# A streaming group softmax on one core: one store gives four of its groups to five small DMAs over unequal partition ranges, and the last three tiles change from 20, 16, 4 to 20, 12, 8 groups

## The chip, the cores and the metric

One core of a Trainium2 chip runs the kernel. The metric is the device time of one execution in microseconds (us); less is better. The kernel before took 1333.27 us, the median of three runs (1332.07 to 1334.61). A further execution was taken by the hardware profiler; all rows shown here come from it.

## The reference

The input is float32 of shape (4, 4096, 4352). Each row of 4352 elements is cut into 8 groups of 544, and a softmax is taken in each group:

```
x_g = x.reshape(B, N, 8, 544)
exp = np.exp(x_g - x_g.max(axis=-1, keepdims=True))
out = exp / exp.sum(axis=-1, keepdims=True)
```

So 285.21 MB are read and as many are written, with little arithmetic on each element.

## The kernel before

The tensor is seen as 131,072 groups of 544 floats (2176 bytes). The 128 partitions hold 1024 groups each, and the work is cut into 44 tiles, numbered 0 to 43. Tiles 0 to 40 give 24 groups to each partition (6528 KB a tile), tile 41 gives 20, tile 42 gives 16 and tile 43 gives 4 (line 35). The groups of one partition are contiguous in DRAM, so a tile's transfer is one run of bytes per partition: 52,224 bytes in a full tile. Four SBUF buffers of 24 groups are used in turn (tile t uses buffer t mod 4), and the results overwrite the input in place.

The stages of a tile:

- **Load** (lines 110 to 117). SyncE issues all loads in the order of the tiles. Tile 0 comes in three loads of 8 groups. From tile 4 on, the load of tile t waits until the store of tile t-4 has fully landed (line 116), since both use the same buffer. Loads go through the queue that the profile calls q1.
- **Compute**. VectorE takes the negated maximum of 8 groups at a time (line 77; 4 at a time in the last three tiles, where `ENDING` and `FINE` apply), for all pieces of a tile. ScalarE then does the exponential of each group with its sum (line 100). VectorE takes the reciprocals of the sums (line 85) and multiplies (line 88), piece by piece. VectorE's order is fixed: all maxima of a tile, then all its products, then the next tile. After a tile's last product it raises the semaphore `scaled`.
- **Store**. GpSimd waits for `scaled` and issues the stores of tiles 0 to 41 (line 124), through the queue that the profile calls q0. SyncE issues the stores of the last two tiles, 42 and 43 (line 120), so these go through q1, behind all loads.

A DMA over 128 partitions is carried by the core's 16 DMA engines. Each engine has its own packets, and sends a 4-byte packet of its own to the completion semaphore when its part is done; the semaphore counts 16 of them for each DMA. A load that waits for a store therefore waits for the slowest of the 16 engines.

Of the kernel before, what the change touches and what calls it, by code (L numbers as in the profile page):

```python
# [1 line left out]

# [4 lines left out]


@with_exitstack
def kernel(  # L10
    ctx: ExitStack,
    tc: tile.TileContext,
    x: bass.AP,
    out: bass.AP,
):
    nc = tc.nc
    G = 8
    P = 128
    C = 8
    NT = 4  # L20
    LAST = 2
    FIRST = (8, 8, 8)
    FINE = 4
    ENDING = 3
    f32 = mybir.dt.float32
    X = mybir.AxisListType.X
    Exp = mybir.ActivationFunctionType.Exp
    xf = x.flatten_outer_dims()
    of = out.flatten_outer_dims()
    N, D = xf.shape  # L30
    Dg = D // G
    per = N * G // P
    T = 3 * G
    sizes = [T] * (per // T - 1)
    sizes += [20, 16, per - sum(sizes) - 36]
    nt = len(sizes)
    turns = (nt - 1) // NT
    start = [sum(sizes[:t]) for t in range(nt + 1)]
    assert start[nt] == per and min(sizes) > 0
    xg_all = xf.rearrange("n (g d) -> (n g) d", d=Dg)  # L40
    og_all = of.rearrange("n (g d) -> (n g) d", d=Dg)

    def dram(a, t):
        lo, hi = start[t] * P, start[t + 1] * P
        return a[lo:hi, :].rearrange("(p g) d -> p (g d)", p=P)

    def parts(t):
        size = C if t < nt - ENDING else FINE
        return [(c, min(c + size, sizes[t])) for c in range(0, sizes[t], size)]

    before = [0]
    for t in range(nt):
        before.append(before[-1] + len(parts(t)))

    landed = [tc.alloc_semaphore(f"landed{b}") for b in range(NT)]
    stored = [tc.alloc_semaphore(f"stored{b}") for b in range(NT)]
    first_landed = [tc.alloc_semaphore(f"first_landed{k}") for k in range(len(FIRST) - 1)]
    last_stored = tc.alloc_semaphore("last_stored")
    max_done = tc.alloc_semaphore("max_done")
    exp_done = tc.alloc_semaphore("exp_done")  # L60
    rec_done = tc.alloc_semaphore("rec_done")
    scaled = tc.alloc_semaphore("scaled")

    ctx.enter_context(tc.tile_critical(  # L64
        sync_engine=mybir.EngineType.Pool, no_gpsimd_drain=True))
    bufs = [ctx.enter_context(nc.sbuf_tensor(f"xt{b}", [P, T * Dg], f32)) for b in range(NT)]
    mx = ctx.enter_context(nc.sbuf_tensor("mx", [P, NT, T], f32))
    sm = ctx.enter_context(nc.sbuf_tensor("sm", [P, NT, T], f32))
    rs = ctx.enter_context(nc.sbuf_tensor("rs", [P, NT, T], f32))

    def groups(b, lo, hi):
        return bufs[b][:, lo * Dg:hi * Dg].rearrange("p (g d) -> p g d", d=Dg)

    def vector_tile(t, landed_at, done):
        b = t % NT
        for k, (lo, hi) in enumerate(parts(t)):
            i = nc.vector.reduce_max(  # L77
                out=mx[:, b, lo:hi], in_=groups(b, lo, hi), axis=X, negate=True)
            if t == 0 and k < len(FIRST) - 1:
                i.wait_op(first_landed[k], 16, "sem-ge")  # L80
            elif t == 0 or k == 0:
                i.wait_op(landed[b], landed_at, "sem-ge")
            i.then_inc(max_done, 1)
        for k, (lo, hi) in enumerate(parts(t)):
            nc.vector.reciprocal(out=rs[:, b, lo:hi], in_=sm[:, b, lo:hi]).wait_op(  # L85
                exp_done, done + k + 1, "sem-ge").then_inc(rec_done, 1)
            xg = groups(b, lo, hi)
            i = nc.vector.tensor_tensor(  # L88
                out=xg, in0=xg,
                in1=rs[:, b, lo:hi].unsqueeze(2).to_broadcast([P, hi - lo, Dg]),  # L90
                op=mybir.AluOpType.mult,
            ).wait_op(rec_done, done + k + 1, "sem-ge")
        i.then_inc(scaled, 1)

    def scalar_tile(t, done):
        b = t % NT
        for k, (lo, hi) in enumerate(parts(t)):
            xg = groups(b, lo, hi)
            for g in range(lo, hi):
                i = nc.scalar.activation(  # L100
                    out=xg[:, g - lo, :], in_=xg[:, g - lo, :], func=Exp,
                    bias=mx[:, b, g:g + 1], scale=1.0, accum_out=sm[:, b, g:g + 1])
                if g == lo:
                    i.wait_op(max_done, done + k + 1, "sem-ge")
            i.then_inc(exp_done, 1)

    def buf(t):
        return bufs[t % NT][:, :sizes[t] * Dg]

    for k, size in enumerate(FIRST):  # L110
        cols = slice(sum(FIRST[:k]) * Dg, sum(FIRST[:k + 1]) * Dg)
        nc.sync.dma_start(out=buf(0)[:, cols], in_=dram(xg_all, 0)[:, cols]).then_inc(  # L112
            first_landed[k] if k < len(FIRST) - 1 else landed[0], 16)
    for t in range(1, nt):
        if t >= NT:
            nc.sync.wait_ge(stored[t % NT], 16 * (t // NT))
        nc.sync.dma_start(out=buf(t), in_=dram(xg_all, t)).then_inc(landed[t % NT], 16)
    for t in range(nt - LAST, nt):
        nc.sync.wait_ge(scaled, t + 1)
        nc.sync.dma_start(out=dram(og_all, t), in_=buf(t)).then_inc(last_stored, 16)  # L120

    for t in range(nt - LAST):
        nc.gpsimd.wait_ge(scaled, t + 1)
        nc.gpsimd.dma_start(out=dram(og_all, t), in_=buf(t)).then_inc(stored[t % NT], 16)  # L124
    for t in range(nt - NT, nt - LAST):
        nc.gpsimd.wait_ge(stored[t % NT], 16 * (t // NT + 1))
    nc.gpsimd.drain()
    nc.gpsimd.wait_ge(last_stored, 16 * LAST)

    nc.scalar.preload_act_table(Exp)  # L130
    turn = before[NT]
    with nc.scalar.Fori(0, turns):
        for t in range(NT):
            scalar_tile(t, before[t])
        nc.scalar.sem_inc(max_done, -turn)
    for t in range(turns * NT, nt):
        scalar_tile(t, before[t] - before[turns * NT])

    for t in range(NT):
        vector_tile(t, 16, before[t])  # L140
    for b in range(NT):
        nc.vector.sem_inc(landed[b], -16)
    nc.vector.sem_inc(exp_done, -turn)
    nc.vector.sem_inc(rec_done, -turn)
    with nc.vector.Fori(1, turns):
        for t in range(NT, 2 * NT):
            vector_tile(t, 16, before[t] - turn)
            nc.vector.sem_inc(landed[t % NT], -16)
        nc.vector.sem_inc(exp_done, -turn)
        nc.vector.sem_inc(rec_done, -turn)  # L150
    for t in range(turns * NT, nt):
        vector_tile(t, 16, before[t] - before[turns * NT])


# [1 line left out]
_INS = ['x']  # L156
_OUTS = [((4, 4096, 4352), 'float32')]


# [23 lines left out]
```

## Time and profile before

| what | value |
|---|---|
| median of three runs | 1333.27 us |
| profiled execution, its own time | 1325.78 us |
| its span, first to last instruction | 1323.5 us |
| bytes read, bytes written | 285.21 MB, 285.21 MB |
| DMA rate over the span | 431 GB/s |
| VectorE busy | 1208.0 us (91%) |
| ScalarE busy | 755.2 us (57%) |
| GpSimd busy | 22.6 us (2%) |

The views used below are these. The page's DMA rows give, in 40 equal slices, the mean busy share of the 16 DMA engines in tenths (9 is 90% or more) and the rate. The chain of waits follows the work that ended last back to the start. The DMA view of a window counts the packets that start in that window; "under 512 B" counts the small ones, which here are the 4-byte completion packets, one per engine and DMA. In a window that is short against a packet, shares and rates can exceed what is possible, because a packet is counted whole where it starts; the counts are what such a window is read for. The timeline lists instructions in order of time: start, duration, engine, line, operation, and in brackets the idle time before it with what ended it. "SPq" is SyncE's queue of DMA issues.

### The profile page before, as it was taken

How to read it: one execution, taken by the hardware profiler on the slowest of the kernel's cores; microseconds unless marked ns; L12 is line 12 of the kernel's file. 1: busy time of each engine (PE TensorE's matmuls, PEld its weight loads, DVE VectorE, ACT ScalarE, POOL GpSimd, SP SyncE). 2: the span in 40 equal slices, each digit the busy share in tenths (PEclk: the TensorE clock that was granted, in tenths of full speed). 3: DMA queues.
4: the chain of work that ended last, by engine and by line, in shares of the span. 5: the costliest groups of instructions: out<-in, count | busy, mean ns of one | idle time of the engine just before them, and what ended most of it. 6: DMA issues, size and time to landing. Idle time of an engine off the chain costs nothing.

```text
span 1323.5 us, 2707 instructions
## 1 busy us (share of the span) xinstructions
DVE 1208.0 (91%) x399; ACT 755.2 (57%) x2049; POOL 22.6 (2%) x46
## 2 busy tenths in 40 slices
DVE  7999999999998999999999999889999999999996
ACT  5556666555555556666665555555566566665553
POOL 0000000000000000000000000000000000000000
DMA  9999999999999999999999999999999999999998
GB/s 404 429 429 430 431 437 436 437 429 431 437 432 439 432 429 432 439 432 436 431 431 440 431 439 429 431 436 437 437 431 431 431 437 434 439 431 429 440 431 362
DMA packets 12964, 570.46 MB, mean 431 GB/s; under 512 B 1440, under 2 KB 1440, under 8 KB 1440
## 3 DMA queue, kind: packets, MB, share of 16 engines
q1 hardware_dynamic: 6912, 290.79, 50.9%
q0 software_dynamic: 6048, 279.64, 48.8%
q14 instruction: 4, 0.03, 0.0%
HBM read 285.21 MB, written 285.21 MB: 431 GB/s over the span
## 4 chain that ended last, share of the span: by engine, by line
DMA 72%; DVE 27%; issue 0%; ACT 0%; SPq 0%; POOLq 0%
DMA out_dram<-xt 36%; DMA xt<-in_x_dram 36%; DVE xt L88 14%; DVE mx L77 13%; DVE rs L85 0%; ACT xt L100 0%; SPq L112 0%; SPq L178 0%; POOLq L64 0%; POOLq L167 0%
## 5 line engine op out<-in xcount | busy, mean ns | idle before, releaser
L100 ACT ACTIVATE xt<-xt,mx 128x544 f32<-128x544 f32 x1024 | 749.8, 733 | 554.8 <-DVE mx L77 554.8
L77 DVE TENSOR_REDUCE mx<-xt 128x8 f32<-128x4352 f32 (+1 forms) x133 | 592.4, 4509 | 98.0 <-DMA xt<-in_x_dram 98.0
L88 DVE TENSOR_TENSOR xt<-xt,rs 128x4352 f32<-128x4352 f32 (+1 forms) x133 | 601.3, 4521 | 4.5
L100 ACT ACTIVATION_READ_ACCUMULATOR xt<-xt,mx 128x1 f32 x1024 | 191.4, 187 | 0.0
L124 POOL DMA_DIRECT2D out_dram<-xt x42 | 22.4, 534 | 1262.6 <-DVE xt L88 1262.6
L85 DVE RECIPROCAL rs<-sm 128x8 f32<-128x8 f32 (+1 forms) x133 | 25.6, 193 | 3.1 <-ACT xt L100 3.1
L130 ACT ACT_TABLE_LOAD x1 | 1.3, 1283 | 0.9 <-PEq L167 0.9
L167 POOL MEMSET const-float32-0.0<- 128x1 f32 x1 | 0.1, 98 | 0.2 <-issue 0.2
L167 POOL MEMSET const-bfloat16-1.0<- 128x1 bf16 x1 | 0.1, 101 | 0.0
L167 POOL MEMSET const-float32-1.0<- 128x1 f32 x1 | 0.1, 98 | 0.0
L167 POOL MEMSET const-uint8-127<- 128x1 uint8 x1 | 0.1, 98 | 0.0
## 6 DMA issues: line engine op xcount, KB each, us to landing
out_dram<-xt POOLq DMA_DIRECT2D x41, 6528.0 KB, 48.4
xt<-in_x_dram SPq DMA_DIRECT2D x40, 6528.0 KB, 46.3
xt<-in_x_dram SPq DMA_DIRECT2D x3, 2176.0 KB, 12.5
xt<-in_x_dram SPq DMA_DIRECT2D x1, 5440.0 KB, 43.8
out_dram<-xt POOLq DMA_DIRECT2D x1, 5440.0 KB, 24.3
xt<-in_x_dram SPq DMA_DIRECT2D x1, 4352.0 KB, 40.0
out_dram<-xt SPq DMA_DIRECT2D x1, 4352.0 KB, 14.0
xt<-in_x_dram SPq DMA_DIRECT2D x1, 1088.0 KB, 29.7
```

The costliest lines, as they stand in the source:

```text
L77: i = nc.vector.reduce_max(out=mx[:, b, lo:hi], in_=groups(b, lo, hi), axis=X, negate=True)
L85: nc.vector.reciprocal(out=rs[:, b, lo:hi], in_=sm[:, b, lo:hi]).wait_op(exp_done, done + k + 1, "sem-ge").then_inc(rec_done, 1)
L88: i = nc.vector.tensor_tensor(out=xg, in0=xg, in1=rs[:, b, lo:hi].unsqueeze(2).to_broadcast([P, hi - lo, Dg]), op=mybir.AluOpType.mult,).w ...
L100: i = nc.scalar.activation(out=xg[:, g - lo, :], in_=xg[:, g - lo, :], func=Exp, bias=mx[:, b, g:g + 1], scale=1.0, accum_out=sm[:, b, g:g ...
L124: nc.gpsimd.dma_start(out=dram(og_all, t), in_=buf(t)).then_inc(stored[t % NT], 16)
L130: nc.scalar.preload_act_table(Exp)
L167: nc = _bacc.Bacc("TRN2", target_bir_lowering=False, num_devices=1)
```

## The change

There are two edits.

The last three tiles hold 20, 12 and 8 groups instead of 20, 16 and 4.

The store of tile 20 is split. The first 20 of its 24 groups go out in one DMA over 128 partitions. The last 4 groups (8704 bytes in each partition) go out in five DMAs over partitions 0 to 1, 2 to 101, 102 to 103, 104 to 105 and 106 to 127. The first four of the five are cut into runs of 2 groups (`max_dma_last_dim`, 4352 bytes); the fifth has runs of 8704 bytes. All six DMAs raise the same semaphore, and the load of tile 24 now waits for all six (`stored_by`).

```diff
+    UNEVEN = (20,)
+    EDGE = 4
+    PIECE = 2
+    SPLITS = ((0, 2), (2, 102), (102, 104), (104, 106))
...
-    sizes += [20, 16, per - sum(sizes) - 36]
+    sizes += [20, 12, per - sum(sizes) - 32]
...
+    def stores_of(t):
+        return 2 + len(SPLITS) if t in UNEVEN else 1
+
+    def stored_by(t):
+        return 16 * sum(stores_of(u) for u in range(t % NT, t + 1, NT))
+
     for t in range(1, nt):
         if t >= NT:
-            nc.sync.wait_ge(stored[t % NT], 16 * (t // NT))
+            nc.sync.wait_ge(stored[t % NT], stored_by(t - NT))
...
     for t in range(nt - LAST):
         nc.gpsimd.wait_ge(scaled, t + 1)
-        nc.gpsimd.dma_start(out=dram(og_all, t), in_=buf(t)).then_inc(stored[t % NT], 16)
+        o, i, done = dram(og_all, t), buf(t), stored[t % NT]
+        if t not in UNEVEN:
+            nc.gpsimd.dma_start(out=o, in_=i).then_inc(done, 16)
+            continue
+        edge = (sizes[t] - EDGE) * Dg
+        nc.gpsimd.dma_start(out=o[:, :edge], in_=i[:, :edge]).then_inc(done, 16)
+        for lo, hi in SPLITS:
+            nc.gpsimd.dma_start(
+                out=o[lo:hi, edge:], in_=i[lo:hi, edge:],
+                max_dma_last_dim=PIECE * Dg * 4).then_inc(done, 16)
+        rest = SPLITS[-1][1]
+        nc.gpsimd.dma_start(out=o[rest:, edge:], in_=i[rest:, edge:]).then_inc(done, 16)
     for t in range(nt - NT, nt - LAST):
-        nc.gpsimd.wait_ge(stored[t % NT], 16 * (t // NT + 1))
+        nc.gpsimd.wait_ge(stored[t % NT], stored_by(t))
```

Where the instructions stand is read in each engine's program. The first place is GpSimd's list of stores (`out_dram<-xt`; the shape is partitions by elements, or partitions by runs by elements). Before, its rows around the stores are:

```order
L178 UNCONDITIONAL_BRANCH
L124 DMA out_dram<-xt 128x13056 x41
L124 DMA out_dram<-xt 128x10880
L112 UNCONDITIONAL_BRANCH
L64 UNCONDITIONAL_BRANCH
```

After the change the same place reads:

```order
L136 DMA out_dram<-xt 128x13056 x20
L139 DMA out_dram<-xt 128x10880
L141 DMA out_dram<-xt 2x2x1088
L141 DMA out_dram<-xt 100x2x1088
L141 DMA out_dram<-xt 2x2x1088 x2
L145 DMA out_dram<-xt 22x2176
L136 DMA out_dram<-xt 128x13056 x20
L136 DMA out_dram<-xt 128x10880
```

One store in the middle of 41 equal ones has become six, and no wait stands between the six.

The second place is the list of SyncE's DMAs, loads (`xt<-in_x_dram`) and the last two stores. Before:

```order
L112 DMA xt<-in_x_dram 128x4352 x3
L117 DMA xt<-in_x_dram 128x13056 x40
L117 DMA xt<-in_x_dram 128x10880
L117 DMA xt<-in_x_dram 128x8704
L117 DMA xt<-in_x_dram 128x2176
L120 DMA out_dram<-xt 128x8704
L120 DMA out_dram<-xt 128x2176
```

After:

```order
L116 DMA xt<-in_x_dram 128x4352 x3
L127 DMA xt<-in_x_dram 128x13056 x40
L127 DMA xt<-in_x_dram 128x10880
L127 DMA xt<-in_x_dram 128x6528
L127 DMA xt<-in_x_dram 128x4352
L130 DMA out_dram<-xt 128x6528
L130 DMA out_dram<-xt 128x4352
```

The order is the same; four groups per partition have moved from tile 42 to tile 43, in the load and in the store. On VectorE tile 42 has three maxima and three products instead of four and four, and tile 43 two and two instead of one and one.

## The prediction

> **What bounds the kernel now.** I read the page's engine rows first, then its DMA rows, then the chain.
>
> ```profile
> DVE 1208.0 (91%) x399; ACT 755.2 (57%) x2049; POOL 22.6 (2%) x46
> DMA  9999999999999999999999999999999999999998
> GB/s 404 429 429 430 431 437 436 437 429 431 437 432 439 432 429 432 439 432 436 431 431 440 431 439 429 431 436 437 437 431 431 431 437 434 439 431 429 440 431 362
> DMA 72%; DVE 27%; issue 0%; ACT 0%; SPq 0%; POOLq 0%
> ```
>
> The 16 DMA engines are busy in every slice; VectorE, the next busiest, is idle for 9% of the span. The DMA view of the stretch from 400 to 1200 us says how busy, and what a packet costs:
>
> ```profile
> DMA packets 7478, 347.14 MB, mean 434 GB/s; under 512 B 831, under 2 KB 831, under 8 KB 831
> q0 software_dynamic: 3743, 173.75, 50.2%
> q1 hardware_dynamic: 3735, 173.39, 50.0%
> ```
>
> 50.2% and 50.0% are all of 16 engines times 800 us. So the kernel is bound by bytes through the engines, and its floor is the work of the engine that has most. 100.2% x 16 x 800 us over 7478 - 831 = 6647 packets of 52,224 bytes is 1.930 us a packet. Since no byte is saved, only two things are left to change: how evenly the engines end, and pauses at the end.
>
> How evenly they end is read from the completion packets ("under 512 B"). Four windows: 1305.2 to 1306.29 and 1308.7 to 1308.8 us (store of tile 41, q0), 1319.3 to 1319.62 and 1321.6 to 1321.7 us (store of tile 43, q1):
>
> ```profile
> DMA packets 14, 0.04 MB, mean 40 GB/s; under 512 B 13, under 2 KB 13, under 8 KB 13
> ...
> DMA packets 2, 0.03 MB, mean 348 GB/s; under 512 B 1, under 2 KB 1, under 8 KB 1
> ...
> DMA packets 16, 0.03 MB, mean 82 GB/s; under 512 B 13, under 2 KB 13, under 8 KB 13
> ...
> DMA packets 1, 0.00 MB, mean 0 GB/s; under 512 B 1, under 2 KB 1, under 8 KB 1
> ```
>
> Thirteen engines finish tile 41 by 1306.25 us, and the last one at 1308.75; the whole kernel ends with the last one alone at 1321.65, two us after the thirteen. The two others, by the same count (one completion each), finish tile 41 in these windows, 1306.6 to 1306.8 and 1308.0 to 1308.2 us:
>
> ```profile
> DMA packets 2, 0.03 MB, mean 174 GB/s; under 512 B 1, under 2 KB 1, under 8 KB 1
> ```
>
> So there are three **late engines**, at 1306.75, 1308.1 and 1308.75. Before the store of tile 42 the thirteen pause: in 1306.44 to 1306.6 us thirteen first packets of q1 start together.
>
> ```profile
> q1 hardware_dynamic: 13, 0.45, 658.1%
> ```
>
> **The change part by part.** First the five extra DMAs. GpSimd issues them after the store of tile 20, here with the next store; the third row is SyncE's issue of the loads of tiles 23 and 24, the second of which ends at 691.99.
>
> ```profile
> 643.35 0.53 POOL L124 DMA_DIRECT2D out_dram<-xt  x1 [30.29 <-DVE xt L88]
> 674.16 0.53 POOL L124 DMA_DIRECT2D out_dram<-xt  x1 [30.28 <-DVE xt L88]
> 660.86 31.13 SPq L117 DMA_DIRECT2D xt<-in_x_dram  x2
> ```
>
> Five more issues at 0.53 us are 2.7 us on GpSimd, inside 30.28 us in which it only waits: nothing. Without that idle time the store of tile 21 would go out 2.7 us later.
>
> The smaller packets: from 1317.9 to 1319.3 us (store of tile 43, 8704 bytes a packet) the engines gave
>
> ```profile
> q1 hardware_dynamic: 65, 0.55, 93.5%
> ```
>
> which is 93.5% x 16 x 1.4 us over 63 data packets, 0.332 us each. With 1.930 us for 52,224 bytes, a packet costs 0.012 us and 36.7 ns for each 1000 bytes. An unsplit row of the last 4 groups then costs 0.32 us within its long packet, as two runs of 4352 bytes 0.34 us, as one of 8704 bytes 0.33 us. No row shows a 4352-byte packet; 0.17 us is an estimate from those two. Spread evenly, 234 more packets x 0.012 us over 16 engines are 0.18 us.
>
> The main term is **who carries the 128 rows**. Before, each engine carries 8 of them, 2.56 us. No row shows a DMA of 2, 22 or 100 partitions. What binds from below: the latest engine can be spared at most its 8 rows, 2.6 us. From above: all 100 rows on one engine are 92 rows more, 92 x 0.34 = 31 us. The nearest rows are the 128-partition DMAs, where all engines used carry equal parts. I take equal parts here too: 100 rows on ten engines (the largest number up to 16 that divides 100) at 10 rows, 2 rows on two engines, 22 rows on eleven at 2 rows. If the first four DMAs use different engines (2 + 10 + 2 + 2 = 16), about ten engines end with up to 12 rows, 10 x 0.34 + 2 x 0.33 = 4.1 us, or 1.55 us more than before; six engines end with 1 to 3 rows, 0.34 to 1.0 us, or 1.55 to 2.2 us less.
>
> The Trainium skill, "DMA: Bandwidth & Descriptors", section "Why a DMA increments its semaphore by 16 and not by 1", gives the dividing rule for the number of engines, but also an exception that speaks against it: some direct copies from GpSimd run on all 16 with the rows rounded up. By the exception 100 rows are 7 on fourteen engines, 2 on the fifteenth, none on the last, and only the last two are clearly spared; no row of this case shows either form.
>
> Next, the **order of packets**. In the window 1286 to 1296 us loads of 8704-byte packets run beside stores of much larger ones, and both queues start about as many packets (q1's 94 hold 16 completions):
>
> ```profile
> q0 software_dynamic: 87, 3.39, 78.3%
> q1 hardware_dynamic: 94, 0.82, 19.3%
> ```
>
> An engine alternates packet by packet. So a small store packet lets a whole load packet of 1.93 us pass. When the store of tile 20 starts, at about 661 us, some 12 load packets are ahead on each engine (half of tile 22, all of 23). Eight go beside the eight long store packets (8 x (1.61 + 1.93) = 28.3 us), four beside the first four small ones (8.4 us), and the other 18 small ones follow alone (3 us): tile 20 is stored at about 701 us where it was 691.5, while load 23 lands 7 to 9 us earlier. Load 24 is issued later, and the load queue may run dry for 4 us. What covers this is the store of tile 21, issued at 674.16 and waiting in q0; no engine stands still, so it costs nothing. Without that cover it would cost those 4 us.
>
> Last, the **tail**. Load and store bytes are the same, four groups move one tile on. VectorE before:
>
> ```profile
> 1285.99 9.40 DVE L77 TENSOR_REDUCE mx<-xt 128x4 f32<-128x2176 f32 x4 [1.35 <-DMA xt<-in_x_dram]
> 1305.49 2.41 DVE L77 TENSOR_REDUCE mx<-xt 128x4 f32<-128x2176 f32 x1
> 1311.00 0.18 DVE L85 RECIPROCAL rs<-sm 128x4 f32<-128x4 f32 x1 [3.10 <-ACT xt L100]
> 1311.22 2.43 DVE L88 TENSOR_TENSOR xt<-xt,rs 128x2176 f32<-128x2176 f32 x1
> ...
> 1273.09 0.33 SPq L117 DMA_DIRECT2D xt<-in_x_dram  x1
> 1305.60 8.41 SPq L120 DMA_DIRECT2D out_dram<-xt  x2
> ...
> xt<-in_x_dram SPq DMA_DIRECT2D x1, 1088.0 KB, 29.7
> ```
>
> Tile 42 ends one maximum (2.35 us) and one product with its reciprocal (2.55) sooner, and starts 1.35 us sooner, since its smaller load has landed: its store is issued at about 1299.4 instead of 1305.60, and the pause of the thirteen goes. Load 43 lands at 1273.09 + 29.7 = 1302.8 at the latest; the wait for it takes the place of the wait for load 42. From there two maxima, eight exponentials and the last product take 2.45 + 8 x 0.73 + 0.2 + 2.6 = 11.1 us, so store 43 is issued at 1313.9, against 1313.7 before. A store started 0.84 us after its issue above (1305.60 to 1306.44), so it can start at 1314.75. An engine that has finished tile 41 at x ends the store of tile 42 (12 groups, 8 x 0.97 us) at x + 7.7. The latest is busy until 1316.4, so its end does not move: for it, nothing; for the thirteen, a pause of up to 1.5 us. Left alone, the tail is worth 0; if the final chain were later by more than 1.7 us, it would set the end.
>
> **The sum.** If the latest two engines are spared, their ends fall to 1308.75 - 1.55 = 1307.2 or less, and the fullest of the others rises to 1306.25 + 1.55 = 1307.8. The engine that ends last then does so 0.95 us earlier, and 20 groups follow for all as before. 1307.8 + 7.7 = 1315.5 is behind 1314.75, so no new pause opens. Forecast: span 1322.55, own time 1324.8. The runs without the profiler took 1333.27, 7.5 us more than the profiled 1325.78, and no row says where; I take the difference over: 1333.27 - 0.95 = **1332.3 us**.
>
> **The rivals.**
>
> - *The latest engine is among the fuller ones* (the other side). It decides as soon as 4 more rows fall on the engine that ends at 1308.75: 1308.75 + 1.55 = 1310.3, price 1.55 us, 1334.8. For it: nothing names that engine, and ten of sixteen are fuller. Against: it needs only to be one of six.
> - *The latest is spared, the second is not.* 1308.1 + 1.55 = 1309.65, price 0.9 us, 1334.2. It holds if the late engines are not neighbours in the engines' numbering, as the spared ones would be. The Trainium skill, same page, section "Latency and other measured facts", says that engines 7 and 15 are usually slower, half the row apart; the trace agrees that a few are late, but does not name them.
> - *The change does not do what it says*: the pieces are spread over all engines about evenly, or rounded up. Price 0.1 to 0.2 us, 1333.4.
> - *The 100 rows fall on few engines.* On five engines 20 rows each, 12 x 0.34 = 4.1 us more: 1306.25 + 4.1 - 1308.75 = 1.6 us, 1334.9, if on-time ones; on a late one 4.1, 1337.4; on one engine 31 us, 1364. For it: no row excludes it; against: every DMA of the trace gives 16 equal parts.
>
> **How the numbers follow.** Latest two spared 0.36, latest fuller 0.18, second fuller 0.16, about even 0.20, few engines 0.05, something unseen 0.05. That spared beats fuller is my judgement, not a row; the six would hold the latest by chance in 6 cases of 16. The best case, all three late engines brought to the thirteen, cannot give more than 1308.75 - 1306.25 = 2.5 us. The three runs lie 1.3 us to each side of their median, and I add that at both ends: 1332.3 - 2.0 = 1330.3, and 1334.8 + 1.3 = 1336.1. About 0.2% (2.7 us) is what a measurement of this kernel can tell from no change. Nearly every case lies within it: same 0.70. Faster takes a full relief and a favourable median, 0.15; slower takes few engines, or the fuller latest and an unfavourable median, 0.15.
>
> **What the new profile would show.** Store of tile 20: completions spread over several us, its last at about 700, load 24 issued then, load 23 landed near 698. If small packets do not alternate one by one, these two move by less than 3 us, and the sum stays. At the end: if spared, the completions of the last store lie closer than 2.2 us, and most engines end together; if the latest is fuller, one engine alone ends 3 us or more after the pack. SyncE issues store 42 by 1300. I am wrong if the engines stand idle anywhere between 690 and 1300 us, or if one engine takes tens of us more than the others.

## The result and the profile after

The changed kernel took 1330.57 us (median of 6 runs, 1329.63 to 1334.75), the kernel before beside it 1332.66 (6 runs, 1326.1 to 1334.61): ratio 1.0001, 95% interval 0.9975 to 1.0028. That is the "same" that was forecast, 1.7 us below the forecast of 1332.3. But two later comparisons of the same pair, with more runs, tell it apart from no change: ratio 1.0028 [1.0010, 1.0047] and 1.0031 [1.0011, 1.0050], so **some 4 us slower** where the prediction worked out 0.95 us faster. The two profiled runs differ by 4.85 us: 1325.78 us before (span 1323.5), 1330.63 after (span 1328.9).

Single runs of one program lie up to 12 us apart, which hid this at first; the section on the experiments shows for one run what made it long. The lowest runs lie closer: 1325.6 to 1326.5 in six sets of runs of the kernel before, 1328.6, 1329.6 and 1329.6 in three sets of the changed one, whose 25 runs hold none below 1328.6.

Where the time went is read first from the page after: its rate by slices of 33.2 us, its packets and its queues.

```profile
GB/s 403 426 429 434 437 432 432 435 434 435 431 435 434 435 431 437 432 432 432 435 423 406 437 434 431 434 437 434 432 431 439 434 432 431 437 435 434 433 428 337
DMA packets 13493, 570.47 MB, mean 429 GB/s; under 512 B 1734, under 2 KB 1734, under 8 KB 1946
```

Two slices in the middle stand out, 423 and 406 (664 to 731 us), where every slice of before between the second and the last but one has 429 or more. The split store starts there. The same stretch in the view by windows, first before, then after; the last two columns are the share of 16 engines that was busy and GB/s:

```profile
660.00:740.00 80.00, 72.47 (x24) 43.20 (x118) 1.59 (x3) 1.00 1.01 436
740.00:1250.00 510.00, 468.53 (x149) 296.10 (x805) 8.50 (x16) 1.00 1.00 434
```

```profile
660.00:740.00 80.00, 69.98 (x23) 42.91 (x118) 1.65 (x3) 1.00 1.00 417
740.00:1250.00 510.00, 467.72 (x149) 293.18 (x797) 8.50 (x16) 1.00 1.00 434
```

After 740 us the rate is the same. Between 660 and 740 us the engines are as busy (1.00) and move 19 GB/s less: (436 - 417) / 434 x 80 us = 3.5 us of the 4.85 by which the two profiled runs differ. Engines that are busy and move less have slower packets; they don't stand idle. Another 1.05 us are at the end: the windows 1323.1 to 1323.5 and 1326.4 to 1326.6 us of after show

```profile
DMA packets 14, 0.02 MB, mean 44 GB/s; under 512 B 13, under 2 KB 13, under 8 KB 13
...
DMA packets 1, 0.00 MB, mean 0 GB/s; under 512 B 1, under 2 KB 1, under 8 KB 1
```

Thirteen engines have ended by 1323.4, the last ends at 1326.5, 3.1 us behind; before it was 2.05 us. So the engines end less evenly than before, not more.

The order of packets changed the way that was predicted. SyncE's issue of load 24 after, then VectorE's maxima:

```profile
703.45 0.33 SPq L127 DMA_DIRECT2D xt<-in_x_dram  x1
```

```profile
703.25 13.86 DVE L81 TENSOR_REDUCE mx<-xt 128x8 f32<-128x4352 f32 x3
...
741.14 4.68 DVE L81 TENSOR_REDUCE mx<-xt 128x8 f32<-128x4352 f32 x1 [9.51 <-DMA xt<-in_x_dram]
```

Load 24 is issued at 703.45 us, when the last piece of store 20 has landed (forecast about 701). Tile 23 is there early (its maxima at 703.25 wait for nothing), and VectorE waits 9.51 us for tile 24. No packet of a load starts from 694.5 to 708.1 us: the load queue is dry for 13.6 us, where the forecast had 4. The store of tile 21 was to cover that.

### The profile page after: what moved, and what is told of

Read it like the earlier page. It is cut to its first block, busy times and chain, and to the rows that moved or that the text cites. A ratio compares the mean times of both kernels' runs of the same rounds, so it can differ in the third digit from the quotient of the medians.

```text
span 1328.9 us, 2712 instructions
## 1 busy us (share of the span) xinstructions
DVE 1207.9 (91%) x399; ACT 755.2 (57%) x2049; POOL 25.8 (2%) x51
## 2 busy tenths in 40 slices
DMA packets 13493, 570.47 MB, mean 429 GB/s; under 512 B 1734, under 2 KB 1734, under 8 KB 1946
## 4 chain that ended last, share of the span: by engine, by line
another core or an unknown queue 42%; DMA 35%; DVE 20%; issue 1%; SPq 1%; ACT 0%; DVEq 0%; POOLq 0%
DMA out_dram<-xt 18%; DMA xt<-in_x_dram 17%; DVE xt L92 10%; DVE mx L81 10%; ACT xt L104 0%; SPq L127 0%; DVE rs L89 0%; SPq L116 0%; DVEq L163 0%; DVEq L166 0%; SPq L199 0%; POOLq L68 0%; DVEq L165 0%; DVEq L164 0%
## 5 line engine op out<-in xcount | busy, mean ns | idle before, releaser
L136 POOL DMA_DIRECT2D out_dram<-xt x41 | 22.0, 537 | 1232.0 <-DVE xt L92 1232.0
L141 POOL DMA_DIRECT2D out_dram<-xt x4 | 2.5, 631 | 0.1
L139 POOL DMA_DIRECT2D out_dram<-xt x1 | 0.5, 531 | 30.2 <-DVE xt L92 30.2
L145 POOL DMA_DIRECT2D out_dram<-xt x1 | 0.5, 545 | 0.0
```

Of the source, the lines that this page charges most:

```text
L136: nc.gpsimd.dma_start(out=o, in_=i).then_inc(done, 16)
L139: nc.gpsimd.dma_start(out=o[:, :edge], in_=i[:, :edge]).then_inc(done, 16)
L141: nc.gpsimd.dma_start(out=o[lo:hi, edge:], in_=i[lo:hi, edge:], max_dma_last_dim=PIECE * Dg * 4).then_inc(done, 16)
L145: nc.gpsimd.dma_start(out=o[rest:, edge:], in_=i[rest:, edge:]).then_inc(done, 16)
```

## The experiments

Four sets; the kernels of a set ran on one chip beside the same runs of the kernel before. The table gives what was measured; the expectations stand with each kernel below.

| kernel | runs | median, lowest us | ratio to before [95%] | GB/s 660 to 740 us | 740 to 1250 |
|---|---|---|---|---|---|
| c1 before again | 10 | 1330.18, 1326.51 | 0.9996 [0.9972, 1.0020] | 435 | 433 |
| e1 tail sizes alone | 10 | 1328.69, 1325.98 | 0.9998 [0.9976, 1.0020] | 435 | 434 |
| e2 split store alone | 10 | 1330.23, 1329.72 | 1.0009 [0.9988, 1.0030] | 420 | 434 |
| e3 small packets, even | 10 | 1329.79, 1326.98 | 0.9994 [0.9969, 1.0018] | 435 | 434 |
| c2 after again | 10 | 1331.65, 1328.62 | 1.0028 [1.0010, 1.0047] | 422 | 433 |
| e4 split at tile 40 | 10 | 1333.13, 1328.73 | 1.0036 [1.0013, 1.0058] | 435 | 434 |
| e5 rows of 8704 bytes | 10 | 1330.69, 1326.67 | 1.0024 [1.0004, 1.0044] | 426 | 433 |
| e6 others spared, tile 40 | 8 | 1331.12, 1329.10 | 1.0034 [1.0007, 1.0061] | 437 | 434 |
| c3 after a third time | 9 | 1332.29, 1329.55 | 1.0031 [1.0011, 1.0050] | 422 | 434 |
| e7 whole rows, 112+8+8 | 4 | 1401.97, 1344.27 | none (one of 1344, three of 1390 to 1414) | 403 | 411 |
| e8 112 rows, edges cut | 4 | 1338.07, 1336.96 | 1.0081 [1.0064, 1.0097] | 412 | 431 |
| e9 as e3, runs set to 2176 bytes | 10 | 1329.37, 1326.30 | 0.9993 [0.9969, 1.0018] | 435 | 434 |

The kernel before had, in the four sets, 31, 29, 14 and 13 runs with medians 1328.21, 1328.16, 1327.65 and 1329.54 us and lowest 1325.64, 1325.74, 1325.84 and 1325.95.

### First set: which half of the change

**c1**: the kernel before, unedited, for the noise.

> This is the kernel before, unchanged, profiled a second time. Theory 'spread' (most of the 5.4 us between the two profiled spans is run-to-run spread of one program): the span of this profile lies anywhere between 1323 and 1333 us, and the rate in the window 660 to 740 us is again about 434 to 436 GB/s. Theories 'order of packets' and 'placement' (below) say nothing against that, but need the window at 434 to 436 GB/s and a distance of about 2 us between the thirteenth and the last engine at the end here too.

Nothing differs, as it must; but its profiled run took 1335.93 us, 10 more than the fastest of the kernel before. The DMA view of 1312.8 to 1318.9 us and of 1318.9 to 1319.3 us shows why:

```profile
DMA packets 33, 1.18 MB, mean 193 GB/s; under 512 B 0, under 2 KB 0, under 8 KB 0
q0 software_dynamic: 3, 0.13, 4.9%
...
q0 software_dynamic: 1, 0.00, 0.1%
```

By 1312.6 us fifteen engines have ended the store of tile 41 (in q0). Then q0 has three data packets in 6.1 us, one behind the other on one engine, whose completion comes at 1319.1: one engine is 6.5 to 9.7 us late, and the end waits for it. So a run's time can hold the accident of one late engine. It isn't the only one: when the load of tile 21 lands, at about 643 us, ahead of any split store's packets, the last engine is 5.4 to 8.7 us behind the first in the profiled runs of c1, c2, c3 and e5 (by the load's 16 completion packets), and at most 3.3 us behind in the ten others. Those four took 1332.7 to 1335.9 us; of the others only e7 and e8 took more than 1331. The rate in the window 660 to 740 us is free of this (435 in c1), and tells a loss of 2 us better than a median of ten runs.

**e1**: the tail sizes alone, all stores plain.

```diff
-    sizes += [20, 16, per - sum(sizes) - 36]
+    sizes += [20, 12, per - sum(sizes) - 32]
```

> Only the sizes 20, 12, 8; every store is one DMA. All theories: 434 to 436 GB/s from 660 to 740 us. The tail moves the store of tile 42 about 6 us earlier, and should leave the end of the latest engine where it was: time within 0.1% of before. If the tail is what hurts (its last chain from the landing of load 43 sets the end), the thirteen engines pause by more than 1 us before the last store and the time is 1 to 3 us longer.

0.9998, and 435 GB/s in the window: the tail neither costs nor gains. Store 42 is issued at 1299.61 us here, as forecast (1299.4).

**e2**: the split store alone; the diff of e1 undone in the changed kernel.

> Only the split store of tile 20; the tail is 20, 16, 4. 'Order of packets' (small store packets each let a long load packet pass, loads run ahead, the load queue runs dry near 700 us and the engines lose some 3 us): about 417 GB/s from 660 to 740 us, as in the changed kernel. 'Placement' (the three late engines are among those that got 12 rows): at the end the last engine is 3.5 us or more behind the thirteenth, against about 2 us before. 'Spread': 434 GB/s in the window and 2 us at the end.

Its ratio doesn't settle it (1.0009, interval from -0.1 to +0.3%), its window does:

```profile
660.00:740.00 80.00, 70.93 (x25) 43.90 (x120) 1.66 (x3) 1.00 1.00 420
```

(436 - 420) / 434 x 80 us = 2.9 us are lost there, and its lowest run is 1329.72, where 18 of the 31 runs of the kernel before are below that. The split alone brings the loss.

**e3**: the last 4 groups in one DMA over all 128 rows, in the same runs of 4352 bytes. Every engine then has 16 small packets.

```diff
-    SPLITS = ((0, 2), (2, 102), (102, 104), (104, 106))
+    SPLITS = ((0, 128),)
...
-        return 2 + len(SPLITS) if t in UNEVEN else 1
+        return 1 + len(SPLITS) if t in UNEVEN else 1
...
-        rest = SPLITS[-1][1]
-        nc.gpsimd.dma_start(out=o[rest:, edge:], in_=i[rest:, edge:]).then_inc(done, 16)
```

> As the changed kernel, but the last 4 groups of tile 20 go out in one DMA over all 128 partitions with the same runs of 4352 bytes: small packets, even shares. 'Order of packets': 16 small packets per engine instead of up to 22 with their completions; the store of tile 20 still lands several us late, and the window 660 to 740 us still shows less than 430 GB/s. 'Placement': the window may be slow, but the last engine ends about 2 us behind the thirteenth as before. If the unequal shares or the unused engines are what slows the window, it is back at 434 GB/s here.

```profile
660.00:740.00 80.00, 74.55 (x26) 44.44 (x122) 1.63 (x3) 1.00 1.01 435
```

Nothing is lost. It isn't the 4352-byte packets as such, and not that they are many; it is something that comes with the pieces over fewer than 128 partitions.

### Second set: the place, the size of the runs, the engines spared

**c2**: the changed kernel again.

> The changed kernel, unchanged, once more. 'Order of packets' and 'placement': the window 660 to 740 us again shows about 417 to 420 GB/s, the lowest runs lie at 1329.6 us or above, some 4 us over the lowest runs of before (1325.6), and the last engine ends 2.5 us or more behind the thirteenth. 'Spread': its lowest runs come down to 1326 to 1327 us and the window is not low every time.

1.0028 [1.0010, 1.0047], 422 GB/s in the window. The change costs 1 to 6 us.

**e4**: the same split on the store of tile 40, whose buffer no load waits for.

```diff
-    UNEVEN = (20,)
+    UNEVEN = (40,)
```

> The same split on the store of tile 40 instead of tile 20. No load waits for that store. 'Order of packets': the late store holds nothing up, the load queue does not run dry, so the 3 us of the window are gone and the lowest runs are at 1327 to 1328 us (1325.6 plus 1.5 for the larger share on the latest engine). 'Placement' alone, without a cost of the order: 1330 us as with tile 20, and 434 GB/s everywhere. The window 660 to 740 us is at 434 to 436 GB/s by every theory.

1.0036, lowest 1328.73: as slow as with tile 20, but by another road. Its windows, then those of e1, which has the same tail:

```profile
660.00:740.00 80.00, 72.19 (x24) 43.71 (x120) 1.59 (x3) 1.00 1.01 435
1250.00:1310.00 60.00, 58.52 (x35) 35.14 (x96) 4.17 (x7) 1.00 1.00 424
```

```profile
660.00:740.00 80.00, 72.41 (x26) 43.90 (x120) 1.60 (x3) 1.00 1.01 435
1250.00:1310.00 60.00, 54.87 (x33) 32.15 (x89) 1.07 (x2) 1.00 0.99 429
```

The stretch at tile 20 is whole again and the one at tile 40 has the dip. It holds only (429 - 424) / 434 x 60 = 0.7 us of the 2.75 between the lowest runs of e4 and e1. The rest lies in how unevenly the engines end: the 16 completions of the last store come from 1318.0 to 1325.6 us in e4 and from 1320.7 to 1322.4 in e1, on average at 1321.0 and 1321.1. With the split at tile 20 the average itself is later: 1323.8 in the changed kernel against e1's 1321.1, and 1323.8 in e2 against 1319.8 before, each pair with the same tail. So e4 doesn't show that the loss at tile 20 comes without a load that is issued late.

**e5**: the pieces in whole rows of 8704 bytes, half as many packets.

```diff
-    PIECE = 2
+    PIECE = 4
```

> As the changed kernel, tile 20, but the last 4 groups go out in one run of 8704 bytes per row: about 15 small packets per engine instead of 28, if the rows fall on the engines as before. 'Order of packets': like the even small packets, 16 per engine, which kept 435 GB/s, the window 660 to 740 us recovers to 430 GB/s or more. If unequal shares or idle engines make the window slow, it stays at 417 to 422. 'Placement': the last engine still ends 2.5 to 3.5 us behind the thirteenth, lowest runs about 1327 us. If two-dimensional pieces are spread over all 16 engines with the rows rounded up, the number of 4-byte packets falls well below the changed kernel's 1734.

```profile
660.00:740.00 80.00, 76.91 (x26) 49.87 (x136) 1.46 (x3) 1.00 1.01 426
```

426 GB/s is 1.8 us lost, and 1.0024: between the changed kernel and before. This isn't a test of the number of packets alone, since the rows also went to other engines. The page counts the 4-byte packets, of before, of after (above) and of e5:

```profile
DMA packets 12964, 570.46 MB, mean 431 GB/s; under 512 B 1440, under 2 KB 1440, under 8 KB 1440
```

```profile
DMA packets 13237, 570.47 MB, mean 428 GB/s; under 512 B 1584, under 2 KB 1584, under 8 KB 1584
```

Five more DMAs have 80 completions. What goes beyond, 1734 - 1440 - 80 = 214 and 1584 - 1440 - 80 = 64, fits to the packet if an engine without a share gets as many 4-byte packets as the others have data packets: 214 = 14 x 2 + 6 x 20 + 14 x 2 + 14 x 2 + 5 x 2 with the pieces on 2, 10, 2, 2 and 11 engines; 64 = 14 + 14 + 14 + 10 + 12 if the 100 whole rows go 7 each to fourteen engines, 2 to the fifteenth and none to the last. So the prediction's equal parts hold for the change, and rounding up, which it set aside there, holds for e5.

**e6**: e4 with six pieces and a rest of 16 partitions, which by the same rule spare other engines (positions 5 to 10 of the 16).

```diff
-    SPLITS = ((0, 2), (2, 102), (102, 104), (104, 106))
+    SPLITS = ((0, 25), (25, 31), (31, 56), (56, 81), (81, 87), (87, 112))
```

> Tile 40 again, with pieces of 25, 6, 25, 25, 6, 25 and 16 partitions. If 25 rows go on five engines and 6 on six, in turn, the six engines 5 to 10 in that order get 3 rows instead of 8 (-1.6 us) and the other ten 11 rows (+1.0 us); in the changed kernel positions 0, 1 and 12 to 15 were spared, and the latest engine was one of positions 2 to 10. 'Placement': with the latest engine spared more often, the last engine ends nearer to the thirteenth than in the run with the changed kernel's pieces on tile 40, and the lowest runs are 1.5 to 2.5 us below that run's. If placement does not matter, both have the same lowest runs within 0.5 us.

1.0034 beside e4's 1.0036, lowest runs 1329.10 and 1328.73. If the loss came from the fuller engine being the late one, sparing others would have moved it by 1.5 to 2.5 us. The lowest runs differ by 0.4 us, and the last store's completions are as far apart (1318.2 to 1326.1 us). But its window is slower than e4's:

```profile
1250.00:1310.00 60.00, 58.53 (x35) 34.03 (x93) 5.47 (x9) 1.00 1.00 417
```

(424 - 417) / 434 x 60 = 1.0 us could hide a gain of that size. So sparing other engines gains no 1.5 us, and nothing can be said below about 1 us.

### Third set: no small packets

**c3**: the changed kernel a third time.

> The changed kernel, a third time, in five rounds, to say whether it is slower than before or the same. 'Order of packets' with 'placement' expects 1.002 to 1.004 times the time of before, lowest runs at 1328.6 to 1329.6 us. 'Spread' expects a ratio within 0.1% of one.

1.0031 [1.0011, 1.0050], as c2.

**e7**: three DMAs of whole rows (52,224 bytes) over 112, 8 and 8 partitions, no small packet at all.

```diff
-    SPLITS = ((0, 2), (2, 102), (102, 104), (104, 106))
+    SPLITS = ((0, 112), (112, 120), (120, 128))
...
+            nc.gpsimd.dma_start(out=o[lo:hi], in_=i[lo:hi]).then_inc(done, 16)
```

> Tile 20 again, but without small runs: the store goes out in three DMAs of whole rows (52,224 bytes), over 112, 8 and 8 partitions. If 112 rows are 7 on each engine and 8 rows are one on each of the first eight engines, both times, eight engines carry 9 rows (+1.93 us) and eight 7 (-1.93 us). Long packets only, so 'order of packets' expects no loss: 430 GB/s or more from 660 to 740 us. 'Placement': the lowest runs are 1.9 us above those of before (1325.7) if the latest engine is among the first eight, so about 1327.6, with the last engine 4 us behind the thirteenth; if it is among the other eight the lowest runs are within 0.5 us of before. If unequal shares by themselves slow the window, it is at 417 to 425 GB/s here too. If the two 8-row DMAs take different halves, nothing differs from before.

The largest loss of all, 1344 to 1414 us; the profiled run is one of the three long ones, 1390.21. The page's rate by slices, then the windows:

```profile
GB/s 409 421 436 431 434 433 433 433 433 433 433 433 435 433 433 433 433 433 435 400 396 412 429 423 429 426 417 430 430 429 417 390 388 397 375 381 362 314 266 325
```

```profile
660.00:740.00 80.00, 65.86 (x23) 44.09 (x120) 1.12 (x2) 1.00 1.00 403
740.00:900.00 160.00, 144.09 (x48) 88.35 (x240) 2.65 (x5) 1.00 1.00 422
900.00:1100.00 200.00, 158.86 (x51) 98.41 (x267) 3.19 (x6) 1.00 0.99 420
1100.00:1250.00 150.00, 121.45 (x39) 78.26 (x214) 2.12 (x4) 1.00 0.94 388
```

Up to 1100 us the engines are as busy as before and carry less, long after the one split store; later they stand idle too. Nothing recovers, though every later DMA is over 128 partitions. What lasts is one late engine: by its completions the load of tile 39 lands on fourteen engines from 1217.4 to 1218.3 us, on one at 1226.5 and on the last at 1252.8, 35 us late, where the load of tile 21, ahead of the split, had all within 3.0 us. Why that engine fell behind isn't shown, nor whether it did in the run of 1344.27. No small packet is needed for the loss in the first window.

**e8**: 112 whole rows, then twice 8 rows, each cut into one group and 23.

```diff
+        nc.gpsimd.dma_start(out=o[:112], in_=i[:112]).then_inc(done, 16)
...
+            for c0, c1 in ((0, Dg), (Dg, sizes[t] * Dg)):
+                nc.gpsimd.dma_start(
+                    out=o[lo:hi, c0:c1], in_=i[lo:hi, c0:c1],
+                    max_dma_last_dim=(c1 - c0) * 2).then_inc(done, 16)
```

> The mirror: 112 whole rows, then for two times 8 rows one group (two runs of 1088 bytes) and 23 groups (two runs of 25,024 bytes). If three-dimensional pieces of 8 rows take eight engines in turn, the two 23-group pieces both fall on the last eight engines: these carry about 8.9 rows (+1.8 us), the first eight about 7.1 (-1.8 us). 'Placement' expects the opposite of the run with the lower half fuller: one of the two has its lowest runs 1.5 to 2 us above the other's, and the one with the latest engine spared ends with less than 1 us between the thirteenth and the last engine. 'Order of packets': 4 more short or half-long packets per engine and queue, so at most 1 us lost in the window 660 to 740 us.

```profile
660.00:740.00 80.00, 70.40 (x23) 43.32 (x118) 1.67 (x3) 1.00 1.00 412
740.00:1250.00 510.00, 460.22 (x146) 285.65 (x777) 8.50 (x16) 1.00 1.00 431
```

1.0081: 412 GB/s are 5 to 10 below the changed kernel's 417 to 422, and the rest runs at 431 instead of 434. Its 4-byte packets don't tell which half of the engines got the fuller share, so it can't say whether the half matters, as it was meant to.

e7 and e8 say something else. From 664 to 684 us the only store under way is their first piece, 112 whole rows. e7's 4-byte packets (1488 = 1440 + 32 completions of two more DMAs + 16) leave no engine without a share of it: the two pieces of 8 rows take the 16, one for each of the 8 engines without a row. So the 112 rows are 7 on each engine. Before, e7 and e8:

```profile
664.00:684.00 20.00, 17.52 (x7) 6.87 (x21) 0.53 (x1) 1.00 1.01 439
...
664.00:684.00 20.00, 16.38 (x7) 5.74 (x17) 0.58 (x1) 1.00 1.00 402
...
664.00:684.00 20.00, 15.97 (x7) 5.32 (x15) 0.58 (x1) 1.00 1.00 397
```

The twelve other profiled runs have 431 to 452 GB/s there. So a piece over 112 partitions slows the packets with equal shares, long packets only, and before any load is issued late.

### Last: the order by itself

One rival was left: in e3 the load queue's gap (8.1 us, from 696.6 to 704.7) is shorter than in the changed kernel (13.6 us). **e9** was to make it longer without uneven shares: e3 with runs of one group.

```diff
-    PIECE = 2
-    SPLITS = ((0, 2), (2, 102), (102, 104), (104, 106))
+    PIECE = 1
+    SPLITS = ((0, 128),)
```

> Even shares, but twice as many small packets: the last 4 groups of tile 20 in one DMA over 128 partitions with runs of 2176 bytes, 32 small packets per engine, as many turns as the changed kernel's 28 and their completions. 'Order of packets' alone: the store of tile 20 lands as late as in the changed kernel, no load packet starts for 10 us or more near 700 us, and the window 660 to 740 us falls to 417 to 424 GB/s; ratio 1.001 to 1.003. 'Rows carried by other engines' (new: what slows the packets is that the pieces are laid on other engines than those that carry these rows in a 128-partition DMA, and that the engines fall out of step): the load queue may run dry just as long, but the window keeps 430 GB/s or more and the time is that of before within 0.1%.

It didn't. The pages of e3 and of e9 count the same packets:

```profile
DMA packets 13236, 570.46 MB, mean 429 GB/s; under 512 B 1456, under 2 KB 1456, under 8 KB 1712
...
DMA packets 13236, 570.46 MB, mean 430 GB/s; under 512 B 1456, under 2 KB 1456, under 8 KB 1712
```

The last 4 groups of 128 rows are in 1712 - 1456 = 256 packets in both, so they have 4352 bytes, 16 on each engine, though runs of 2176 were set. e9 is e3 once more: load 24 is issued at 700.88 us (e3 701.06), the gap is 8.2 us, and the time is again that of before. The window, then the DMA view of 690 to 720 us of e9 and of after:

```profile
700.88 0.33 SPq L127 DMA_DIRECT2D xt<-in_x_dram  x1
```

```profile
660.00:740.00 80.00, 74.52 (x26) 43.98 (x120) 1.60 (x3) 1.00 1.01 435
```

```profile
DMA packets 503, 12.77 MB, mean 426 GB/s; under 512 B 33, under 2 KB 33, under 8 KB 279
```

```profile
DMA packets 742, 11.87 MB, mean 396 GB/s; under 512 B 303, under 2 KB 303, under 8 KB 514
```

So a load queue that is dry for 8 us costs nothing that shows, while the store of tile 21 is there. For the 13.6 us of the changed kernel that is not shown. There is a sign that the gap has a part. These are the first sixteen load packets behind it, in after (708 to 711.3 us) and in e9 (704.5 to 706.7 us):

```profile
q1 hardware_dynamic: 16, 0.84, 88.5%
...
q1 hardware_dynamic: 16, 0.84, 92.8%
```

Sixteen packets and a share of 16 engines make 88.5% x 3.3 us = 2.92 us a packet in after, and 92.8% x 2.2 us = 2.04 us in e9, where 1.93 is usual: 0.99 us lost on each engine against 0.11.

## Why the prediction was right or wrong

**GpSimd: right.** The five issues lie in its waiting time, which for the store of tile 21 falls from 30.28 to 27.19 us:

```profile
643.01 0.53 POOL L139 DMA_DIRECT2D out_dram<-xt  x1 [30.21 <-DVE xt L92]
643.62 2.52 POOL L141 DMA_DIRECT2D out_dram<-xt  x4
646.13 0.55 POOL L145 DMA_DIRECT2D out_dram<-xt  x1
673.86 0.58 POOL L136 DMA_DIRECT2D out_dram<-xt  x1 [27.19 <-DVE xt L92]
```

**More packets: not contradicted.** 0.18 us would not be seen, and e3 and e9 show no loss; a packet of 4352 bytes usually takes 168 ns there (0.17 us forecast). **Equal parts: right**, by the 214 fill packets. The dividing rule of the Trainium skill, "DMA: Bandwidth & Descriptors", section "Why a DMA increments its semaphore by 16 and not by 1", agrees with this count, and its exception with e5's 64.

**The order of packets: right in direction, too small in size, its price open.** Load 24 is issued at 703.45 us (forecast about 701), but the load queue is dry for 13.6 us, not 4. The step "no engine stands still, so it costs nothing" holds for the gap of 8 us in e3 and e9. In the changed kernel no engine stood still either, but the first packets behind the gap were slow, 0.99 us on each engine, and the step had no term for that.

**The tail: right, worth 0** (e1). In the changed kernel the store of tile 42 is issued at 1302.19 instead of the forecast 1299.4 (e1 1299.61), since everything runs later:

```profile
1302.19 15.31 SPq L130 DMA_DIRECT2D out_dram<-xt  x2
```

**Who carries the rows: here the prediction failed.** The step was "ten engines end with up to 12 rows, 10 x 0.34 + 2 x 0.33 = 4.1 us, or 1.55 us more than before", and behind it "If the latest two engines are spared". It priced a row at 0.34 us whichever engine carries it and whatever the others do. Each engine's packets can be followed through the trace, as each starts where the last one ended. The time of its packets beyond the usual price (the most frequent time of a size, 1.928 us for 52,224 bytes), averaged over the 16 engines, between 660 and 740 us: before 0.01 us, e9 0.26, e3 0.35, e5 1.60, e2 2.48, after 2.42, of which 0.63 lies in the small packets and 1.79 in long ones. Of its 212 packets of 4352 bytes 30 took over 200 ns, sixteen of them 311 to 346 ns, about twice the usual 168. Of the 1.79 us only 0.24 are in packets that start by 703.1 us, when the last piece has ended; 0.42 are in store packets behind that and 1.12 in load packets, most of it in the first sixteen of load 24. The other three traces of this split (e2, c2, c3) have 1.5 us behind the last piece too. So the piece that failed is one that no row of the profile before could show: when a store is cut over fewer than 128 partitions, packets get slower, its own and long ones of both queues, and most of the time lost in long ones is lost when its pieces are done. In place of -0.95 us the runs have some +4 (c2 +3.5 and c3 +4.6 between the medians).

**"Latest two spared": not so.** In the profiles of the changed kernel and of e2, the engine that was latest before the split is, by its count of small packets, one of the fuller, and the end is 3.1 us wide. This was the rival "the latest engine is among the fuller ones", priced at 1.55 us. But the end explains only about 1 us of the profiled 4.85; the other 3.5 are lost around the split. The sum had also left out the third late engine: had only that one been fuller, 1306.75 + 1.55 = 1308.3 us would have left 0.45 of the 0.95 us.

**The range** was to hold 1330.57, and did; the later medians, 1331.65 and 1332.29, lie in it too. What it was put around was wrong: 1333.27, the median of the three runs shown, was high by chance; the later sets of 13 to 31 runs have 1327.65 to 1329.54. The forecast's error in sign and this offset nearly cancelled, so that it came within 1.7 us is luck. The 7.5 us that it carried over between profiled and other runs were spread of single runs: the lowest runs without the profiler are at 1325.6 too.

**What stays open** is why pieces over fewer than 128 partitions slow packets. In a transfer to 128 partitions, says the Trainium skill, same page, section "The descriptor swizzle", each engine writes one SBUF port of its own. If stores read it in the same way, a piece that hands rows to other engines could put two engines at a port. The 112 rows of e7 and e8, slow with equal shares, fit that, but no trace names engines or ports, so it is argued and not shown. It would not explain the packets that are slow behind the last piece. For these the dry load queue is a rival: no run on tile 20 had such pieces without a late load 24, or even shares with a gap of over 8.2 us. And why one engine of e7 falls 35 us behind isn't known.

## What to carry to other kernels

A store cut into pieces over few partitions, to even out the ends of engines that are all busy, cost more (2.4 to 3.5 us around the pieces) than the unevenness that it was to remove (2 us); even 112 whole rows, 7 on each engine, lowered the rate from 439 to some 400 GB/s while they went out. Smaller packets over all 128 partitions cost nothing that could be measured. When every engine is busy, price a DMA not only by its own packets: look at the rate of the stretch around it, which showed 3 to 4% in one profile when medians of ten runs, with up to 12 us between runs of a program, did not show 0.3%. Count in the trace what an edit made before reading its time: e9's packets were those of e3. And before working with differences of 1 us, get the lowest of many runs: a median of three was some 4 us off.

## What the runs showed of the hardware that was not expected

- A piece over 112 partitions, 7 whole rows on each engine, lowered the rate to 402 and 397 GB/s (e7, e8) where twelve other profiled runs have 431 to 452.
- Runs set to 2176 bytes (e9) went out as packets of 4352, and runs set to 1088 bytes (e8) as sixteen packets between 2 and 8 KB, one a row (its page has 1553 packets under 2 KB and 1569 under 8 KB).
- Engines without a share of a GpSimd DMA were handed 4-byte packets, as many as the others have data packets: 214 in the changed kernel, 64 in e5.
- A piece of 100 rows of two runs each went to ten engines at 10 rows; the same 100 rows in one run each, to fourteen at 7 and one at 2 (e5). Both are read from the counts of 4-byte packets.
- One store of whole rows in 112 + 8 + 8 partitions made 1326 us into 1344 to 1414; in the profiled run of 1390 one engine fell 35 us behind, and the rate from 1100 to 1250 us was 388 instead of 434 GB/s.
- From the issue of load 24 at 703.45 us to its first packet at 708.1 passed 4.6 us, and thirteen of its sixteen first packets took more than 1.93 us, up to 4.07.
- A single late engine (6.5 to 9.7 us in c1) made a run 10 us longer than the fastest. Leaving e7 and e8 aside, the four profiled runs above 1331 us had an engine 5.4 us or more behind at 643 us, the eight others none above 3.3; unprofiled runs aren't shown.
